# Modulation rows on the vector engine, and a written order in attention

## The chip, the cores and the metric

The kernel runs on one core of a Trainium2 chip. The core has five engines that work side by side, each on its own stream of instructions: TensorE (PE), which multiplies matrices and transposes, VectorE (DVE), ScalarE (ACT), GpSimd (POOL), and SyncE (SP), which issues the loads and stores. The metric is the device time of one execution in microseconds.

## The reference, cut to what matters

One layer over 1024 latent tokens of width 1024, with a context of 256 tokens. A conditioning vector gives six modulation rows; the layer is windowed attention beside a short convolution, an output projection with a gated residual, and a mixture of 16 experts in which each expert picks its 128 best tokens.

```python
mod = silu(c) @ w_ada + b_ada                     # six rows of 1024: sh1 sc1 gt1 sh2 sc2 gt2
h = rmsnorm(x, g_mix) * (1 + sc1) + sh1
q, k, v, bg, cg, hv = split(h @ w_in)
q, k = rope(q), rope(k)
att = softmax([sink, q @ k_ctx, q @ k_window] / 8) @ [v_ctx, v_window]
conv = bg * conv3(cg * hv)
x = x + gt1 * (concat(att, conv) @ w_out)
h2 = rmsnorm(x, g_ffn) * (1 + sc2) + sh2
x = x + gt2 * expert_choice_moe(h2)
out = rmsnorm(x, g_final)
```

## The kernel before, in words

**Stages.** First the rows sh1 and sc1 are computed for the latent and the context from 8 MB of `w_ada` (L230 on). Then the tokens are normalized and transposed and multiplied by the key/value weights, then by the query weights. Attention and the convolution run together; the output projection follows, tile by tile of 128 tokens, with the routing of the tile before beside it; then come the 16 experts, whose weights are 192 MB, and the last norm. Every fp32 operand of a large matrix product is split into a rounded high half and the rest as a low half, and three products of halves stand for one.

**Key/value and query projections.** `build_hT` (L281) transposes a strip of 128 columns of up to four token tiles on PE, applies the modulation and splits the result. For odd strips ACT applies the modulation and DVE makes both halves; for even ones DVE applies it, ACT makes the high half and POOL, or DVE for some, the low one (L289 to L297). `kv_stream` (L410) runs 24 builds, 8 for the context and 16 for the latent, and multiplies each strip three steps later (`proj_kv`, L311). `q_stream` (L524) then runs eight query tiles of 24 matmuls each (`q_proj`, L495); a tile's result is rotated (`rotary`, L320, lines 327 to 334, on DVE), its high half is made by ACT (L509) and its low half by DVE (L510). PE transposes a finished tile (`q_turn`, L513) behind the sixth step, that is the 18th matmul, of the next. The two streams of keys are transposed within the second tile (`turn_later`, L374).

**Later modulation rows.** Beside these projections `mod_stream` (L466) computes the other four rows, r = 0 to 3 for gt1, sh2, sc2 and gt2. For each row and each of 8 strips of the input it loads 512 KB of `w_ada`, ACT multiplies by the strip's silu values (L461) and POOL adds into a sum (L463). The sums over partitions are PE products with selecting columns (L473), and the four rows go to memory (L490).

**Attention.** A unit is one block of 128 queries and two heads, 32 units in all. `scores` (L551) multiplies, adds the mask while taking the maximum (L575), scales the maximum by -1/8 (L577), takes the exponential on ACT with its sum (L578), and treats the sink apart with small operations (L585 to L588) before it scales by the reciprocal (L592, L594). `values` (L599) transposes the probabilities of the unit before, splits them (L625, L626), multiplies them with the values and joins two halves of the result (ACT at L639, DVE at L643). `conv` (L714) runs 12 weight blocks of 16 steps; a block's weights are loaded one block ahead and split by ACT and POOL (L710, L711), and the three taps are computed on POOL and ACT (L755 to L760). `prepare` (L798) loads, gates and splits the first output weights.

**What sets the order.** `weave` (L69) takes the next piece of the stream that is furthest behind its share of a total, each yield being a piece's weight; that is the order in which instructions are written. PE executes as written everywhere. DVE, ACT, POOL and SP are ordered by a planner with its own simulated clock, except in stretches that are marked as written by hand, the end of the output projection for one. Every engine takes its instructions one after another: one that waits holds those behind it.

**Memory.** A pool of 21 large slots is handed out by `slots.get` and `slots.put`; a load waits for the last reader of its slot. Tiles named `wm` have three buffers in turn.

## Time and profile before

| | |
|---|---|
| median of 3 runs | 1163.87 us (1163.16 to 1164.9) |
| profiled execution | 1163.48 us, span 1161.7 us |
| PE, DVE, ACT, POOL busy | 91%, 83%, 66%, 30% of the span |
| granted clock, mean | 0.965 |
| DMA | 292.89 MB, mean 252 GB/s |

The span runs from the first to the last instruction; 1.78 us lie around it. Busy shares are means over stages. The granted clock is a share of TensorE's full speed of 2.4 GHz; its other level, 0.50, is 1.2 GHz. The page shows it by slices of 29 us:

```profile
PE   6786889999899998999399999999999999999981
DVE  7888455887878785389899999999999999999975
POOL 0457681221303031222212433322333322330022
PEclk9897999999999999999599999999999999999996
GB/s 376 232 164 144 164 146 19 24 33 1 55 1 37 19 278 339 181 127 270 273 322 356 399 403 390 391 388 389 395 404 392 389 389 389 394 404 390 203 195 221
```

Each digit is a busy share in tenths. The first slices are the modulation and the projections, the seventh to the fourteenth attention, the fifteenth to the nineteenth the output projection, the rest the experts and the end.

### The profile page before, as it was taken

How to read it: one execution, taken by the hardware profiler on the slowest of the kernel's cores; microseconds unless marked ns; L12 is line 12 of the kernel's file. 1: busy time of each engine (PE TensorE's matmuls, PEld its weight loads, DVE VectorE, ACT ScalarE, POOL GpSimd, SP SyncE). 2: the span in 40 equal slices, each digit the busy share in tenths (PEclk: the TensorE clock that was granted, in tenths of full speed). 3: DMA queues.
4: the chain of work that ended last, by engine and by line, in shares of the span. 5: the costliest groups of instructions: out<-in, count | busy, mean ns of one | idle time of the engine just before them, and what ended most of it. 6: DMA issues, size and time to landing. Idle time of an engine off the chain costs nothing.

```text
span 1161.7 us, 15615 instructions
## 1 busy us (share of the span) xinstructions
PE 1058.4 (91%) x5486; PEld 873.5 (75%) x5486; DVE 967.2 (83%) x1661; ACT 766.1 (66%) x1058; POOL 351.0 (30%) x292
## 2 busy tenths in 40 slices
PE   6786889999899998999399999999999999999981
PEld 2675667888788877888288888888888888888861
DVE  7888455887878785389899999999999999999975
ACT  7565655767666643232288878878878877888853
POOL 0457681221303031222212433322333322330022
PEclk9897999999999999999599999999999999999996
DMA  9644440010101079648789999999999999999555
GB/s 376 232 164 144 164 146 19 24 33 1 55 1 37 19 278 339 181 127 270 273 322 356 399 403 390 391 388 389 395 404 392 389 389 389 394 404 390 203 195 221
DMA packets 90790, 292.89 MB, mean 252 GB/s; under 512 B 7044, under 2 KB 20816, under 8 KB 89688
## 3 DMA queue, kind: packets, MB, share of 16 engines
q1 hardware_dynamic: 84808, 270.40, 61.0%
q0 software_dynamic: 5904, 21.50, 7.7%
q8 instruction: 43, 0.70, 0.2%
q14 instruction: 35, 0.29, 0.1%
HBM read 266.69 MB, written 25.18 MB: 251 GB/s over the span
## 4 chain that ended last, share of the span: by engine, by line
PE 72%; DVE 13%; issue 5%; ACT 4%; DMA 4%; POOL 1%; POOLq 0%; ACTq 0%; DVEq 0%; SPq 0%
PE pg L1313 14%; PE pu L1313 14%; PE py L1313 13%; PE po L879 7%; PE ps_cv L731 3%; PE ps_cv L730 3%; PE ps_cv L732 3%; PE pt L622 2%; PE po_att L613 2%; DVE whl L1150 2%; PE ps_s L565 2%; PE xTp L1299 1%; PE ps_s L563 1%; PE pl L954 1%; PE hTtp L1299 1%
## 5 line engine op out<-in xcount | busy, mean ns | idle before, releaser
L1150 DVE TENSOR_TENSOR whl<-raw,whl 128x1024 fp32r<-128x1024 f32 x384 | 455.2, 1224 | 29.9 <-ACT whl L1147 18.9
L1147 ACT CAST whl<-raw 128x1024 fp32r<-128x1024 f32 x384 | 400.2, 1054 | 100.2 <-PE pu L1313 35.6
L1313 PE MATMUL pg<-whl,xT 128*128 128x512 f32 x768 | 186.2, 395 | 2.1 <-DVE whl L1150 2.1
L1313 PE MATMUL pu<-whl,xT 128*128 128x512 f32 x768 | 180.9, 392 | 0.0
L1313 PEld LDWEIGHTS pg<-whl,xT 128*128 128x128 f32 x768 | 142.3, 189 | 31.6 <-DVE whl L1150 2.9
L1313 PE MATMUL py<-whl,hTt 128*128 128x512 f32 x720 | 165.9, 389 | 0.0
L1313 PEld LDWEIGHTS pu<-whl,xT 128*128 128x128 f32 x768 | 143.0, 188 | 29.4
L1313 PEld LDWEIGHTS py<-whl,hTt 128*128 128x128 f32 x720 | 135.1, 188 | 28.4 <-DVE whl L1150 0.3
L1278 POOL TENSOR_SCALAR oh<-iota,pos 128x128 bf16<-128x128 f32 x104 | 100.5, 981 | 0.5
L1371 POOL DMA_INDIRECT acc_d<-yt,idx x15 | 38.5, 2565 | 196.0 <-DVE yt L1359 196.0
L1323 POOL DMA_INDIRECT xr<-h_d,idx x16 | 22.3, 1395 | 199.2 <-DVE gate_w L1289 199.2
L730 PE MATMUL ps_cv<-hTh,wcs 128*128 128x512 f32 x192 | 81.5, 424 | 0.0
L463 POOL TENSOR_TENSOR acc<-acc,wmod 128x1024 f32<-128x1024 f32 x28 | 70.0, 2518 | 27.8 <-ACT wmod L461 26.7
L625 ACT CAST pth<-pt 128x512 fp32r<-128x512 f32 (+1 forms) x88 | 46.1, 524 | 46.2 <-PE pt L622 46.1
L731 PE MATMUL ps_cv<-hTl,wcs 128*128 128x512 f32 x192 | 76.1, 397 | 0.0
L732 PE MATMUL ps_cv<-hTh,wcs 128*128 128x512 f32 x192 | 76.0, 396 | 0.0
L879 PE MATMUL po<-woh,ah 128*128 128x512 f32 x240 | 70.8, 404 | 0.6 <-ACT woh L223 0.6
L626 DVE TENSOR_TENSOR pth<-pt,pth 128x512 fp32r<-128x512 f32 (+1 forms) x88 | 53.9, 613 | 20.1 <-ACT pth L625 19.2
L711 POOL TENSOR_TENSOR wcs<-wcr,wcs 128x1024 fp32r<-128x1024 f32 x12 | 28.6, 2389 | 110.2 <-ACT wcs L710 87.5
L578 ACT ACTIVATE sm<-sm,negm 128x640 f32<-128x640 f32 (+1 forms) x64 | 51.6, 807 | 4.0 <-DVE negm L577 3.9
L575 DVE CUSTOM_DVE_ANT_0 sm<-ps_s,maskt,sink 128x640 f32<-128x640 f32 (+1 forms) x56 | 48.3, 863 | 6.9 <-PE ps_s L565 6.3
L879 PEld LDWEIGHTS po<-woh,ah 128*128 128x128 f32 x240 | 44.1, 191 | 9.4 <-ACT woh L223 1.0
(297 smaller groups left out, 1828.4 us busy)
## 6 DMA issues: line engine op xcount, KB each, us to landing
raw<-in_w_gate_dram SPq DMA_DIRECT2D x64, 1024.0 KB, 9.6
raw<-in_w_up_dram SPq DMA_DIRECT2D x64, 1024.0 KB, 7.8
raw<-in_w_down_dram SPq DMA_DIRECT2D x64, 1024.0 KB, 9.6
wmod<-in_w_ada_dram SPq DMA_DIRECT2D x32, 512.0 KB, 3.7
wa<-in_w_ada_dram SPq DMA_DIRECT2D x8, 1024.0 KB, 5.3
wcr<-in_w_in_dram SPq DMA_DIRECT2D x12, 512.0 KB, 3.8
xt<-in_x_dram SPq DMA_DIRECT2D x4, 1024.0 KB, 20.6
wor<-in_w_out_dram SPq DMA_DIRECT2D x4, 1024.0 KB
```

Source lines behind the costliest of these rows:

```text
L463: nc.gpsimd.tensor_tensor(acc, acc, wt, op=OP.add)
L575: nc.vector.tensor_tensor_reduce(dst, src, mk, op0=OP.add, op1=OP.max, scale=1.0, scalar=sink8[:, h:h + 1], accum_out=mx[:, b, h:h + 1])
L578: nc.scalar.activation(sm, sm, AF.Exp, bias=negm[:, b, h:h + 1], scale=0.125, accum_out=esum[:, b, h:h + 1])
L626: nc.vector.tensor_tensor(pth[:, 1, :n], pt[:, :n], pth[:, 0, :n].bitcast(F32), op=OP.subtract)
L730: mm(ps, wsp[:, 0, k], hi, start=k == 0, stop=False)
L731: mm(ps, wsp[:, 0, k], lo, start=False, stop=False)
L732: mm(ps, wsp[:, 1, k], hi, start=False, stop=k == KC - 1)
L879: mm(po[n], a, wo[k // 4, n][j][:, k % 4], start=first, stop=last)
L1147: nc.scalar.copy(w[:, 0], t[:, k % 2])
L1150: low = nc.vector.tensor_tensor(w[:, 1], t[:, k % 2], w[:, 0].bitcast(F32), op=OP.subtract)
L1278: nc.gpsimd.tensor_scalar(oh[:, t], iota1, pos[:, t, 0, e:e + 1], None, op0=OP.is_equal)
L1313: mm(ps[n], a_hl[:, a, k], w[:, j, n * 512:(n + 1) * 512], start=first, stop=last)
```

## The change: what it does

The four later rows are computed with one DVE instruction per piece, which multiplies by the strip's silu value and adds to the sum (`mod_add`); POOL and ACT no longer take part. The four are taken apart: sh2 and sc2 stay beside the projections (`mod_stream`), each of their 16 loads with a dependence on the low half of the last finished query tile; gt1 is computed within attention in 24 pieces of 384 or 256 columns, summing in PSUM (`mod_attention`); gt2 is computed in the output projection of tiles 1 to 4, in 16 pieces of 512 columns (`last_row`). The sums over partitions are products with a column of ones, and the bias is added to a column form (`mod_sums`, `mod_row`); sc2's row already holds (1 + sc2) g_ffn.

In the projections, ACT now does both the modulation and the high half of every build, and DVE the low half; the low halves of the key/value weights move from POOL to DVE. The queries are scaled by -1/8 in the instructions of their split, so that attention takes a minimum and no scaled copy. In attention the sink is a further column of the scores, so its operations apart fall away; the join of a unit is written behind the first scores of the unit after the next; DVE and ACT now run as written, as PE does. The convolution's weights are split in halves between the steps of the block before, by ACT and DVE, and the taps are one ACT and two DVE instructions; POOL has no part in either. The first output weights are loaded apart from their gating.

```diff
@@ -265,7 +266,7 @@
     for i in range(2):
         ks = slice(4 * i, 4 * i + 4)
         nc.scalar.copy(wkv_h[:, ks], wkv_r[:, ks])
-        nc.gpsimd.tensor_tensor(wkv_l[:, ks], wkv_r[:, ks], wkv_h[:, ks].bitcast(F32), op=OP.subtract)
+        nc.vector.tensor_tensor(wkv_l[:, ks], wkv_r[:, ks], wkv_h[:, ks].bitcast(F32), op=OP.subtract)
@@ -286,15 +287,9 @@
...
+        nc.scalar.activation(hf, ps[:, :n], AF.Identity, scale=mscale[:, k, j:j + 1], bias=mshift[:, k, j:j + 1])
+        nc.scalar.copy(hi, hf)
+        nc.vector.tensor_tensor(lo, hf, hi.bitcast(F32), op=OP.subtract)
@@ -451,43 +446,94 @@
...
+    def mod_add(src, k, acc, out=None):
+        if k == 0:
+            nc.vector.tensor_scalar(acc, src, silu_c[:, 0:1], None, op0=OP.mult)
+        else:
+            nc.vector.scalar_tensor_tensor(acc if out is None else out, src, silu_c[:, k:k + 1], acc, op0=OP.mult,
+                                           op1=OP.add)
...
+    def mod_sums(pr, acc, r, k0=0):
+        n = acc.shape[1] // 128
+        for q in range(n):
+            mm(pr[:, q:q + 1], acc[:, q * 128:(q + 1) * 128], ones_f, start=True, stop=True)
+        c = 8 * r + k0
+        v = modv[:, c:c + n]
+        nc.vector.tensor_tensor(v, pr[:, 0:n], badaT[:, c:c + n], op=OP.add)
+        if r == 2:
+            nc.vector.scalar_tensor_tensor(v, v, 1.0, gffnT[:, k0:k0 + n], op0=OP.add, op1=OP.mult)
...
+    def mod_row(pr, r):
+        nc.tensor.transpose(pr[:8, :128], modv[:, 8 * r:8 * r + 8], ident)
+        row = w4("prow", (128,))
+        nc.scalar.copy(row[:8], pr[:8, :128])
+        nc.sync.dma_start(rows_d[r].rearrange("(k p) -> k p", p=128), row[:8])
...
+    def mod_stream():
...
+        yield 22
+        acc, s_acc = slots.get((2, D), F32, "acc")
...
+        for i in range(len(items) + 2):
+            if i < len(items):
+                k, r = items[i]
+                st_[i] = wm("wmod")
+                ld = mod_load(st_[i], r, k, slice(0, D))
+                if q_split:
+                    tc.add_manual_dep(ld.ins, q_split[-1].ins.name,
+                                      mybir.DependencyInfo(mybir.DependencyClass.Sync, mybir.DependencyReason.DATA),
+                                      reason="order")
+            if i > 1:
+                k, r = items[i - 2]
+                mod_add(st_.pop(i - 2), k, acc[:, r - 1])
             yield 1
...
+        yield 1
+        pr = p2(0, "prow")
+        for r in (1, 2):
+            mod_sums(pr[:, r - 1], acc[:, r - 1], r)
+        slots.put(s_acc)
+        for r in (1, 2):
+            mod_row(pr[:, r - 1], r)
...
+    def mod_attention(accp):
...
+        stage = work.tile([128, 2, 384], F32, tag="early", name="stage")
+        cols = (slice(0, 384), slice(384, 768), slice(768, 1024))
+        items = [(n, k) for n in range(3) for k in range(KC)]
...
+        yield 4
+        for i, (n, k) in enumerate(items):
+            w = cols[n].stop - cols[n].start
+            src = stage[:, i % 2, :w]
+            last = k == KC - 1
+            mod_add(src, k, accp[:, :w], src if last else None)
+            if last:
+                yield 1
+                mod_sums(accp, src, 0, cols[n].start // 128)
+            load(i + 2)
+            yield 1
+        mod_row(p1(3, "prow"), 0)
@@ -506,9 +552,12 @@
...
+        nc.scalar.activation(qs[:, :, 0, :], tv, AF.Copy, scale=-0.125)
+        low = nc.vector.scalar_tensor_tensor(qs[:, :, 1, :], tv, -0.125, qs[:, :, 0, :].bitcast(F32), op0=OP.mult,
+                                       op1=OP.subtract)
         qs_of[t] = qs
+        q_split.append(low)
...
-    weave([(urgent(steps(kv_stream(), q_stream())), 95.0), (mod_stream(), 56.0)])
+    weave([(urgent(steps(kv_stream(), q_stream())), 95.0), (mod_stream(), 42.0)])
@@ -554,7 +602,15 @@
...
+        def exp(i):
+            h = 2 * hp + i
+            sx = sm2[:, i, :W + 1]
+            nc.scalar.activation(sx, sx, AF.Exp, bias=mx[:, b, h:h + 1], scale=-1.0,
+                                 accum_out=esum[:, b, h:h + 1])
@@ -572,20 +628,17 @@
...
-            nc.vector.tensor_tensor_reduce(dst, src, mk, op0=OP.add, op1=OP.max, scale=1.0,
+            if i == 0:
+                nc.vector.tensor_copy(sm2[:, :, W], sink8[:, hs])
+            nc.vector.tensor_tensor_reduce(dst, src, mk, op0=OP.add, op1=OP.min, scale=1.0,
                                            scalar=sink8[:, h:h + 1], accum_out=mx[:, b, h:h + 1])
-            nc.vector.tensor_scalar(negm[:, b, h:h + 1], mx[:, b, h:h + 1], -0.125, None, op0=OP.mult)
-            nc.scalar.activation(sm, sm, AF.Exp, bias=negm[:, b, h:h + 1], scale=0.125,
-                                 accum_out=esum[:, b, h:h + 1])
             if i == 0:
-                yield
...
-        r = rec[:, b, hs]
-        nc.vector.tensor_tensor(r, sinkb[:, hs], negm[:, b, hs], op=OP.add)
-        nc.scalar.activation(r, r, AF.Exp)
-        nc.vector.tensor_tensor(r, r, esum[:, b, hs], op=OP.add)
-        nc.vector.reciprocal(r, r)
+                exp(0)
+            yield
+        exp(1)
+        yield
+        nc.vector.reciprocal(rec[:, b, hs], esum[:, b, hs])
@@ -633,16 +688,20 @@
...
+        def join():
...
+            up = work.tile([64, 2, 128], F32, tag="up", name="up")
+            nc.scalar.copy(up.rearrange("p b c -> p (b c)"), po[64:128])
+            pov = po.rearrange("p (b c) -> p b c", b=2)
+            for par in range(2):
+                dst = attT[b // 4][0][64 * par:64 * par + 64, hp, (b % 4) * 128:(b % 4 + 1) * 128]
+                nc.vector.tensor_tensor(dst, pov[:64, par], up[:, par], op=OP.add)
...
+        joined.append(join)
@@ -687,12 +736,24 @@
...
+            next(sc, None)
+            while joined:
+                joined.pop()()
+            yield 1
+            next(va, None)
+            yield 1
+            next(sc, None)
+            yield 1
+            next(va, None)
+            next(sc, None)
+            yield 1
+            if u == 0:
+                yield 1
+            next(va, None)
+            next(sc, None)
+            yield 1
+            next(va, None)
+        joined.pop()()
@@ -700,24 +761,33 @@
...
+        if i < 12:
...
+            raw = wm("wcr", (8, 128))
+            c0 = conv_col[part] + f * 128
+            nc.sync.dma_start(raw, win_v[:, :, c0:c0 + 128])
+            conv_w_of[i] = [raw, *slots.get((2, 8, 128), F32R, "wcs")]
+    def conv_split(i, low, n):
+        if i < 12:
+            raw, wsp, _ = conv_w_of[i]
+            ks = slice(4 * n, 4 * n + 4)
+            if low:
+                nc.vector.tensor_tensor(wsp[:, 1, ks], raw[:, ks], wsp[:, 0, ks].bitcast(F32), op=OP.subtract)
+            else:
+                nc.scalar.copy(wsp[:, 0, ks], raw[:, ks])
@@ -730,7 +800,16 @@
...
+                    at = 8 * half + k
+                    if at in (7, 8, 9, 10):
+                        conv_split(i + 1, *divmod(at - 7, 2))
+                    if part == 2 and at in (1, 4):
+                        j = 1 if at == 1 else 2
+                        nc.vector.scalar_tensor_tensor(st["y"], st["u"][:, j:j + S], convT_w[:, 4 * j + f:4 * j + f + 1],
+                                                       st["y"], op0=OP.mult, op1=OP.add)
+                    if k < KC - 1:
+                        yield 1
@@ -751,13 +831,7 @@
...
-                nc.gpsimd.tensor_scalar(y, u[:, 0:S], convT_w[:, f:f + 1], None, op0=OP.mult)
-                tap = wm("tap", (S,))
-                for j in (1, 2):
-                    w = convT_w[:, 4 * j + f:4 * j + f + 1]
-                    nc.scalar.activation(tap, u[:, j:j + S], AF.Copy, scale=w)
-                    nc.gpsimd.tensor_tensor(y, y, tap, op=OP.add)
+                nc.scalar.activation(y, st["u"][:, 0:S], AF.Copy, scale=convT_w[:, f:f + 1])
@@ -800,19 +881,25 @@
...
+        wo_issue(0)
+        yield 5
+        wo_issue(1)
+        wo_gate(0)
+        attended(0, ((0, 4),))
         yield 4
         wo_split(0)
...
+        yield 5
+        wo_issue(2)
+        wo_gate(1)
+        attended(0, ((4, 2),))
+        yield 4
         wo_split(1)
...
-        wo_load(2)
...
+    pb = p2(1, "po_att")
+    with tc.manual_schedule(engines={ET.PE, ET.DVE, ET.Activation}):
+        weave([(steps(attention(), prepare()), 160.0), (conv(), 161.0), (mod_attention(pb[:, 1]), 45.0)])
@@ -829,9 +916,6 @@
...
-    gf = wm("gf")
-    bcast_row(gf, g_ffn[0])
-    nc.vector.scalar_tensor_tensor(S2, S2, 1.0, gf, op0=OP.add, op1=OP.mult)
@@ -1183,6 +1267,33 @@
...
+    def last_row():
+        mem, s_ = slots.get((4, 512), F32, "gt2")
+        items = [(n, k) for n in range(2) for k in range(KC)]
...
+        for i in range(3):
+            load(i)
+        yield 6
+        for i, (n, k) in enumerate(items):
+            mod_add(mem[:, 1 + i % 3], k, mem[:, 0])
+            load(i + 3)
+            if k == KC - 1:
+                yield 1
+                mod_sums(p1(1, "prow"), mem[:, 0], 3, 4 * n)
+            yield 1.8
+        mod_row(p1(1, "prow"), 3)
+        slots.put(s_)
@@ -1190,13 +1301,22 @@
...
+    def last_row_part():
+        c = 0.0
+        while c < 10:
+            w = next(lrow)
+            c += w
+            yield w
...
-        beside(t, [[0.0, before(t)]])
+        lr = [[0.0, last_row_part()]] if 1 <= t < 5 else []
+        beside(t, [[0.0, before(t)]] + lr)
```

## Rows read from the trace of the kernel before

**Rows 1.** Windows view: stretch, us, busy PE, PEld, DVE, ACT, POOL, PEclk, DMA share, GB/s.

```profile
44.50:91.40 46.90, 39.64 (x287) 36.57 (x286) 38.76 (x49) 29.47 (x45) 23.50 (x14) 0.93 0.45 146
91.40:172.80 81.40, 63.96 (x288) 49.38 (x287) 50.19 (x71) 45.71 (x63) 59.06 (x25) 0.92 0.50 162
178.50:420.00 241.50, 234.21 (x1405) 201.94 (x1406) 184.65 (x503) 160.80 (x342) 48.20 (x20) 0.99 0.12 38
420.00:455.00 35.00, 31.52 (x135) 25.40 (x134) 30.91 (x26) 14.20 (x19) 9.33 (x5) 0.95 0.92 350
455.00:540.00 85.00, 85.00 (x455) 72.20 (x453) 54.67 (x258) 23.04 (x54) 22.91 (x46) 1.00 0.62 173
```

**Rows 2.** The waits view, 91.4 to 172.8 us: total, times, longest, in us.

```profile
PE pq L520 <- DVE qs L510: 13.1, 5, 4.6
```

**Rows 3.** The timeline of DVE, query stage: start, us, line, operation.

```profile
128.91 2.60 DVE L334 TENSOR_TENSOR t<-t 128x256 f32<-128x256 f32 x1
132.19 2.07 DVE L510 TENSOR_TENSOR qs<-t,qs 128x512 fp32r<-128x512 f32 x1 [0.68 <-ACT qs L509]
150.39 0.41 DVE L334 TENSOR_TENSOR t<-t 128x256 f32<-128x256 f32 x1
162.07 0.69 DVE L510 TENSOR_TENSOR qs<-t,qs 128x512 fp32r<-128x512 f32 x1 [0.74 <-ACT qs L509]
```

**Rows 4.** The timeline of POOL over the first two of those instructions.

```profile
126.29 7.42 POOL L463 TENSOR_TENSOR acc<-acc,wmod 128x1024 f32<-128x1024 f32 x3 [5.72 <-ACT wmod L461]
```

**Rows 5.** The lines view by form, 55 to 195 us: busy, mean ns, idle before.

```profile
L463 POOL TENSOR_TENSOR acc<-acc,wmod 128x1024 f32<-128x1024 f32 x28 | 70.0, 2518 | 27.8 <-ACT wmod L461 26.7 <-PE ps_q L503 0.5 <-ACT vx L343 0.5
```

**Rows 6.** The same view, 44.5 to 91.4 us, steps of the transposed build.

```profile
L290 ACT ACTIVATE hfs<-ps_xt,mshift,mscale 128x512 f32<-128x512 f32 x4 | 3.1, 776 | 0.0
L296 ACT CAST hTh<-hfs 128x512 fp32r<-128x512 f32 x4 | 2.4, 610 | 5.7 <-DVE hfs L294 5.7
L202 ACT ACTIVATE junk<-xt 128x1024 f32<-128x1024 f32 x3 | 3.2, 1056 | 0.3 <-POOL hcTl L297 0.3
L292 DVE TENSOR_TENSOR hTl<-hfs,hTh 128x512 fp32r<-128x512 f32 x4 | 5.1, 1285 | 0.1
```

**Rows 7.** The timeline of all engines, 30 to 37 us.

```profile
30.40 5.07 POOL L268 TENSOR_TENSOR wkvl<-wkvr,wkvh 128x1024 fp32r<-128x1024 f32 x2 [0.88 <-ACT wkvh L267]
31.14 2.08 DVE L254 TENSOR_TENSOR pmTv<-mparts 128x32 f32<-128x32 f32 x1
36.52 0.69 PE L286 MATMUL ps_xt<-ident,cxt 128*128 128x128 f32 x2 [4.71 <-DVE hf L294]
```

**Rows 8.** The timeline of PE, query stage.

```profile
162.81 1.09 PE L520 MATMUL pq<-ident,qs 128*128 128x128 f32 x8 [2.59 <-DVE qs L510]
163.66 0.48 PE L501 MATMUL ps_q<-wqh,hTh 128*128 128x512 f32 x1
164.21 0.39 PE L503 MATMUL ps_q<-wqh,hTl 128*128 128x512 f32 x1
164.44 0.40 PE L501 MATMUL ps_q<-wqh,hTh 128*128 128x512 f32 x1
```

**Rows 9.** The lines view by form, attention, 178 to 425 us.

```profile
L577 DVE TENSOR_SCALAR negm<-mx 128x1 f32<-128x1 f32 x64 | 9.8, 152 | 2.0
L585 DVE TENSOR_TENSOR rec<-sinkb,negm 128x2 f32<-128x2 f32 x32 | 9.0, 282 | 1.0
L587 DVE TENSOR_TENSOR rec<-rec,esum 128x2 f32<-128x2 f32 x32 | 12.0, 376 | 5.2 <-ACT rec L586 4.5
L626 DVE TENSOR_TENSOR pth<-pt,pth 128x512 fp32r<-128x512 f32 x64 | 44.1, 690 | 19.4 <-ACT pth L625 18.5
```

**Rows 10.** The waits of DVE, attention.

```profile
DVE attT L643 <- ACT up L639: 10.4, 15, 1.5
```

**Rows 11.** The page's costliest groups and its DMA issues.

```profile
L1150 DVE TENSOR_TENSOR whl<-raw,whl 128x1024 fp32r<-128x1024 f32 x384 | 455.2, 1224 | 29.9 <-ACT whl L1147 18.9
wmod<-in_w_ada_dram SPq DMA_DIRECT2D x32, 512.0 KB, 3.7
```

More of the change, by code (lines that the diff above doesn't have):

```diff
@@ L597, in tile_layer @@
     ptf = [0]
+    joined = []
     def values(u):
@@ L634, in values @@
             flush()
-        if b // 4 not in attT:
-            attT[b // 4] = slots.get((4, 512), F32, "attT")
-        up = work.tile([64, 2, 128], F32, tag="up", name="up")
-        nc.scalar.copy(up.rearrange("p b c -> p (b c)"), po[64:128])
-        pov = po.rearrange("p (b c) -> p b c", b=2)
-        for par in range(2):
-            dst = attT[b // 4][0][64 * par:64 * par + 64, hp, (b % 4) * 128:(b % 4 + 1) * 128]
-            nc.vector.tensor_tensor(dst, pov[:64, par], up[:, par], op=OP.add)
-        if b % 2 and hp == 3:
-            slots.put(qT[b // 2][1])
+        def join():
+            if b // 4 not in attT:
+                attT[b // 4] = slots.get((4, 512), F32, "attT")
+            up = work.tile([64, 2, 128], F32, tag="up", name="up")
[4 more added lines that the diff above has]
+                nc.vector.tensor_tensor(dst, pov[:64, par], up[:, par], op=OP.add)
+            if b % 2 and hp == 3:
+                slots.put(qT[b // 2][1])
+        joined.append(join)
     rt = {}
@@ L1184, in order_now, with load @@
         yield
+    def last_row():
+        mem, s_ = slots.get((4, 512), F32, "gt2")
+        items = [(n, k) for n in range(2) for k in range(KC)]
+        def load(i):
+            if i < len(items):
+                n, k = items[i]
+                mod_load(mem[:, 1 + i % 3], 3, k, slice(n * 512, n * 512 + 512))
+        for i in range(3):
[5 more added lines that the diff above has]
+            if k == KC - 1:
+                yield 1
+                mod_sums(p1(1, "prow"), mem[:, 0], 3, 4 * n)
+            yield 1.8
+        mod_row(p1(1, "prow"), 3)
+        slots.put(s_)
+        while True:
+            yield 99
+    lrow = last_row()
     def before(t):
```

154 lines of the change are left out of this document (49 added, 105 removed).

## The prediction

> **What bounds the kernel now.** I read the windows by stage first, then PE's waits, then the timelines of DVE and POOL where PE waits. The reader is to see three kinds of stretch. Beside the key/value and query projections PE is busy for 39.64 of 46.9 and 63.96 of 81.4 us, at a granted clock of 0.93 and 0.92; it falls to 1.2 GHz after the idle stretches [rows 1]. In attention it is busy for 234.21 of 241.5 us, in the output projection for 85.00 of 85.0. So only the projections have much to give, some 25 us of idle PE and the slow clock besides; attention has 7.3 us, the transition behind it 3.5.
>
> The waits say what holds the queries: PE's transposes of a finished query stand for its low half on DVE, 13.1 us in 5 waits [rows 2]. The timelines say why that half is late. The same additions and subtractions take 0.41 and 0.69 us in one query, 2.60 and 2.07 in another [rows 3], and over the long ones POOL runs three additions of the modulation rows [rows 4], 28 of them at 2518 ns [rows 5]. The same shows ahead of the stage: a DVE addition of 32 columns takes 2.08 us while POOL subtracts for 5.07, and PE then stands 4.71 us [rows 7].
>
> **The change part by part.** Terms are for the profiled execution, 1163.48 us (span 1161.7 and 1.78 around it), 0.39 under the median of 1163.87.
>
> *Start.* The key/value weights' low halves move from POOL to DVE. Their two subtractions of 1024 columns cost DVE 2 x 1.22 us [rows 11], behind the modulation's small operations, so those get their short durations back: about 4 us of the 4.71 [rows 7]. That does not pass through, because ACT now does both steps of every transposed build. With 0.78 and 0.61 us for 512 columns [rows 6], I estimate two thirds of 1.39, 0.9 us, for the context's 256. Eight of them and eight squares of 1.06 [rows 6] are 15.7 us from about 31.9 (4 us ahead of the build that feeds PE at 36.52), so the latent builds reach ACT at 47.6, and PE's transposes lead that by 1.6: 46, which is 1.5 later than the 44.5 of now.
>
> *Key/value projection, 44.5 to 91.4.* DVE keeps one subtraction per build (now 1285 ns where POOL is beside it [rows 6], else 0.69 [rows 3]); POOL has none and the modulation adds start later. ACT's builds come to 16 x 1.39 = 22.2 us, under PE's work. PE at 2.4 GHz: a transpose takes (163.66 - 162.81)/8 = 0.106 us, a 512-column matmul 0.23 from start to start [rows 8], a 256-column one half of it, 0.115. Sixteen builds of 4 transposes and 12 matmuls are 28.9 us, the last three context steps 2.1, eight key transposes 0.85: 31.9. Of today's 7.3 us of idle PE I leave 4, for ACT's chain. End: 46 + 31.9 + 4 = 82, against 91.4.
>
> *Query projection.* PE has 192 matmuls (43.9), seven turns of 8 transposes (6.0) and 32 key transposes (3.4), 53.3 us. The next query's 18 matmuls before a turn cover 4.1 us. Without POOL the chain of a query is two products from PSUM at 0.69 (the PSUM form of [rows 9]), two additions at 0.41 [rows 3], 0.61 on ACT [rows 6] and 0.69: 3.5 us and some handing over, so it just fits. New on DVE are 16 multiply-adds of 1024 columns; the trace has none, the nearest row of the same size is 1.22 us [rows 11], and I bound one between 0.7 (a 512-column form [rows 9]) and 2.5 (POOL's). Replaying the two streams by their yields puts load 0 in query 1, load 15 in query 6 and the last add in query 7, two or three per query. A rotary or a subtraction that finds one ahead of it is late by up to 1.2, so I take 0.9 per turn, 6 us in seven; and 5 for the key transposes, asked for 8 us after the last projection while DVE works through four key blocks. If all is hidden this is 0, if every turn meets two adds it is 17. Stage: 82 + 53.3 + 11 = 146.3.
>
> The tail to the first score takes 5.7 us now, from the end of the query window at 172.8 to 178.5. Then it is 16 one-column matmuls, two small additions, two transposes and two copies in a row, each waiting on the one before; I keep 5 (bounds 2 and 9). Attention starts at 151.3: **-27.2**. On SP each load stands behind a query's split and holds what is queued behind it, the next load and lastly the first convolution weights; these are wanted only behind the first score.
>
> One rule speaks against this part. The Trainium skill (Perfetto Trace Analysis, Optimizing Scalar/DVE Operations) says that work of a saturated DVE can go to ScalarE or even GpSimd, and warns that the port these two share may spoil it. Taken by its first half, bringing 16 adds of 1.22 us back would lift DVE's 50.19 us in the query stage [rows 1] to 69.7, about 5 us over the stage forecast, and the sum would be 1143. The trace sides with the warning: most of a long subtraction was time spent beside POOL [rows 3, 4].
>
> *Attention, 178.5 to 420.* DVE loses 64 scalings of the maximum (9.8 us) and two small operations per unit (9.0 and 12.0): 30.8 [rows 9]. It gains 24 weight subtractions of 512 columns at 0.69 (16.6), 8 convolution taps at 1.22 (9.8), 32 sink columns at 0.15 (4.8) and 24 adds of row 0, which I take at 0.5 between a small form's 0.15 and 0.69 (12): 43.2. Net +12 on 184.65 of 241.5 us [rows 1], so DVE has room; ACT's count hardly moves. PE's gain is at most its 7.3 us idle. Against that DVE and ACT now run as written: the joining additions stand for ACT's copy, and that copy behind an exponential (today 10.4 us in 15 waits, longest 1.5 [rows 10]). Bounds -6 and +40; I take **+2**, nearest to today's waits. Loads of row 0 have 10 us each to land in 3.7 [rows 11].
>
> *Transition, 420 to 455.* Output weights are loaded a step ahead of their gating and splitting; PE idles 3.5 us here [rows 1]. Bounds -3.5 and +3: **-2**.
>
> *Output projection, 455 to 540.* PE has no idle here, so each of its waits counts. It gains 8 one-column matmuls and a transpose; DVE gains 16 adds of 512 columns, 16 x 0.69 = 11 on 54.67 of 85 us. Their loads, 256 KB each, go through SP among the expert weights, at a DMA share of 0.62, three ahead. Hidden under PE's matmuls; if a load is late, PE stands at one of two sums and DVE at its add, with the residual queued behind. Bounds 0 and +15: **+1**. The expert stage's own code is not touched; it only moves.
>
> *At nothing.* Some 40 more lines of 512 B among the first small loads are 0.1 us at the 376 GB/s of the first slice. The query's factor and sign ride in instructions that are there anyway. One row less is loaded and multiplied behind attention (1.2 us of DVE, beside PE's first projection).
>
> Sum: 1163.48 - 27.2 + 2 - 2 + 1 = 1137.3, some 1138 on the scale of the median.
>
> **The rivals.**
> *Full cover.* PE never waits beside the projections: 46 + 31.9 + 53.3 + 5 = 136.2, which is -42.3; with -3.6 in attention and -3.5 behind it, 1114. For it: 3.5 of chain under 4.1 of cover, and no POOL. Against: 16 adds in the same DVE stream.
>
> *Late loads hold DVE.* An add whose load is released only by the query's split waits for landing, 3.7 us [rows 11], and the rotary stands behind it: 3.7 in place of 0.9 in seven turns is 19.6 more, 1157. For it: DVE takes its instructions one after another. Against: each add is written two loads behind its own load.
>
> *Attention becomes DVE's (slower).* Per unit of 33, DVE has 196.9/33 = 5.97 us of work. If it also stands 1.5 for the copy behind the exponential [rows 10], 0.6 for the transposed probabilities (today 18.5 us over 33 [rows 9]) and 0.5 for the second exponential before its reciprocal, a unit takes 8.57 against PE's 7.32: +41 us, 1176. It loses to today from 8.2 us a unit. For it: the written order. Against: PE runs ahead only as far as two buffers, and now waits little.
>
> *The moved rows collide.* Row 3's loads land late between 1 MB weight loads, and PE pays the +15 above: 1151.
>
> **How the numbers follow.** Forecast 0.64, full cover 0.13, late loads 0.12, slower attention 0.06, collision 0.05. 1118 to 1158 leaves out the slower case and about half of the full cover. A measurement of this kernel can tell about 0.2%, 2.3 us. All cases but the slower attention lie below that bound; for thin margins of late loads I put 0.03 on no change: faster 0.91, same 0.03, slower 0.06.
>
> **What would show it.** The first score near 151 us with POOL nearly idle before it, the subtraction of the queries at 0.69 in all eight, a granted clock near 1.00 between 82 and 146, and attention still 240 to 246 us long confirm the steps. A wait of DVE's multiply-add for its load in most queries shows the late loads; PE idle of more than 15 us in attention, released by DVE, shows the slower case. The forecast is wrong if attention starts later than 160 or takes over 255.

## The result, and the profile after

The changed kernel takes 1208.78 us (median of 4 runs, 1205.17 to 1211.85) against 1163.8 for the kernel before on the same chip: ratio 1.0384, interval 1.0354 to 1.0414. It is slower, and the forecast of 1138 was wrong in sign.

I cut both profiled executions (1205.17 us with a span of 1203.4, which is 3.6 us under its median; 1163.48 with 1161.7) at the same events. Times in us:

| stretch | before | after | difference |
|---|---|---|---|
| to the last key/value product | 90.8 | 86.3 | -4.5 |
| to the last query product | 81.6 | 73.8 | -7.8 |
| to the first score | 6.1 | 6.7 | +0.6 |
| attention, to the first output product | 255.2 | 299.3 | +44.1 |
| output projection | 116.6 | 126.9 | +10.3 |
| routing, experts, last norm | 611.4 | 610.4 | -1.0 |

The windows of the changed kernel follow, from its first transpose of a latent tile; columns as in [rows 1]. The last line is attention in the kernel before, cut at the same events.

```profile
46.30:86.30 40.00, 35.98 (x284) 34.68 (x284) 22.23 (x36) 30.53 (x52) 1.20 (x2) 0.96 0.14 51
86.30:160.10 73.80, 59.36 (x282) 48.39 (x282) 45.33 (x86) 20.02 (x39) 0.00 (x0) 0.93 0.38 128
166.80:466.10 299.30, 265.18 (x1481) 222.87 (x1482) 194.27 (x465) 161.91 (x321) 2.24 (x13) 0.96 0.17 55
178.50:433.70 255.20, 247.91 (x1466) 213.26 (x1467) 197.96 (x509) 164.93 (x345) 56.76 (x23) 0.99 0.15 50
```

POOL is empty beside the query projections, as meant, and yet PE idles there for 14.4 us at a clock of 0.93. In attention PE, DVE and ACT all idle, PE for 34 us: none of them is full, so they stand for each other. Of the 44.1 us that attention lost, 26.8 are idle PE and 17.3 a PE that is busy for longer, at a granted clock of 0.96 where it had 0.99. The waits of attention (166.8 to 466 us) say where:

```profile
ACT sm L611 <- DVE mx L634: 75.6, 51, 3.9
DVE attT L700 <- ACT up L696: 42.1, 32, 1.4
...
ACT pth L680 <- PE pt L677: 24.3, 26, 3.5
```

Before, ACT stood mostly for PE's transposes, and the copy for the joining additions cost DVE 10.4 us [rows 10]. ACT's wait before, 178.5 to 433.7 us:

```profile
ACT pth L625 <- PE pt L622: 46.1, 50, 2.5
```

Now ACT stands at its exponentials for DVE's maximum. A unit has two of them, one per head: 51.8 of the 75.6 us stand at the first and 23.8 at the second. The timeline of ACT, and then that of DVE, show a first exponential at 217.45, a second at 223.71 and the first of the next unit at 229.97:

```profile
217.45 0.83 ACT L611 ACTIVATE sm<-sm,mx 128x641 f32<-128x641 f32 x1 [1.36 <-DVE mx L634]
...
218.40 0.37 ACT L696 COPY up<-po_att 64x256 f32<-64x256 f32 x1
...
219.85 1.08 ACT L680 CAST pth<-pt 128x512 fp32r<-128x512 f32 x2
223.71 0.83 ACT L611 ACTIVATE sm<-sm,mx 128x641 f32<-128x641 f32 x1 [2.79 <-DVE mx L634]
...
224.54 0.35 ACT L680 CAST pth<-pt 128x256 fp32r<-128x256 f32 x1
...
229.97 0.83 ACT L611 ACTIVATE sm<-sm,mx 128x641 f32<-128x641 f32 x1 [3.63 <-DVE mx L634]
```

```profile
218.80 0.58 DVE L700 TENSOR_TENSOR attT<-po_att,up 64x128 f32<-64x128 f32 x2 [1.39 <-ACT up L696]
...
221.07 0.61 DVE L457 SCALAR_TENSOR_TENSOR po_att<-stage,silu_c,po_att 128x384 f32<-128x384 f32 x1
221.60 1.28 DVE L809 SCALAR_TENSOR_TENSOR cg<-u,smallT,cg 128x1024 f32<-128x1024 f32 x1
222.79 0.88 DVE L634 CUSTOM_DVE_ANT_0 sm<-ps_s,maskt,sink 128x640 f32<-128x640 f32 x1
...
224.93 0.42 DVE L681 TENSOR_TENSOR pth<-pt,pth 128x256 fp32r<-128x256 f32 x1 [0.64 <-ACT pth L680]
...
225.93 0.62 DVE L457 SCALAR_TENSOR_TENSOR po_att<-stage,silu_c,po_att 128x384 f32<-128x384 f32 x1
...
229.04 0.88 DVE L634 CUSTOM_DVE_ANT_0 sm<-ps_s,maskt,sink 128x640 f32<-128x640 f32 x1 [1.24 <-PE ps_s L621]
```

For the second exponential the scores were ready, but DVE had an addition of row 0 and a convolution tap ahead of the maximum. So that exponential came at 223.71, and the 0.35 us copy of transposed probabilities behind it only at 224.54, though PE had made the transposes (0.44 us from 221.21) nearly three microseconds earlier. DVE's subtraction, an addition of row 0 and then PE's value products followed in a chain. PE's timeline has the end of it:

```profile
221.21 0.44 PE L677 MATMUL pt<-ident,sm 128*128 128x128 f32 x2 [0.47 <-DVE pth L681]
...
226.69 1.25 PE L668 MATMUL po_att<-pth,vx 128*128 128x256 f32 x6 [3.45 <-DVE po_att L457]
```

PE multiplies the next scores only behind these products, so the next maximum came at 229.04 and the first exponential that stands for it at 229.97. Behind a first exponential, as at 217.45, wait the joining copy (218.40), at which DVE then stands with all its later work (218.80), and the first copies of transposed probabilities (219.85).

Beside the query projections the rows read otherwise. DVE waits for the loads of its additions, and PE for the low halves of the queries (waits, 86.3 to 160.1 us):

```profile
DVE acc L457 <- DMA wmod<-in_w_ada_dram: 10.3, 5, 3.9
...
PE pq L569 <- DVE qs L557: 14.4, 7, 3.9
```

One turn in DVE's timeline, and the transposes of PE that it releases:

```profile
107.38 0.69 DVE L557 SCALAR_TENSOR_TENSOR qs<-t,qs 128x512 fp32r<-128x512 f32 x1
112.01 1.29 DVE L457 SCALAR_TENSOR_TENSOR acc<-wmod,silu_c,acc 128x1024 f32<-128x1024 f32 x1 [3.94 <-DMA wmod<-in_w_ada_dram]
113.21 0.68 DVE L322 TENSOR_TENSOR t<-ps_q,ropet 128x512 f32<-128x512 f32 x1
...
114.41 1.28 DVE L457 SCALAR_TENSOR_TENSOR acc<-wmod,silu_c,acc 128x1024 f32<-128x1024 f32 x1
115.60 0.42 DVE L328 TENSOR_TENSOR t<-t 128x256 f32<-128x256 f32 x1
...
116.27 1.28 DVE L457 SCALAR_TENSOR_TENSOR acc<-wmod,silu_c,acc 128x1024 f32<-128x1024 f32 x1
117.47 0.68 DVE L557 SCALAR_TENSOR_TENSOR qs<-t,qs 128x512 fp32r<-128x512 f32 x1
```

```profile
118.30 1.94 PE L569 MATMUL pq<-ident,qs 128*128 128x128 f32 x8 [3.55 <-DVE qs L557]
```

Two or three loads are released by one split and land together; DVE stands for the first with the rotary behind it, and the other two additions sit inside the rotary. The window from 110 us is the landing, at a DMA share of 0.94. PE's idle then costs clock (windows of 4 us): 0.59 is a mixture of the levels 1.2 and 2.4 GHz, and the eight transposes above take 1.94 us where a turn at full clock takes 1.06.

```profile
110.00:114.00 4.00, 4.00 (x19) 3.29 (x19) 1.99 (x3) 0.00 (x0) 0.00 (x0) 1.00 0.94 357
114.00:118.00 4.00, 0.75 (x4) 0.29 (x2) 4.00 (x6) 0.63 (x1) 0.00 (x0) 0.99 0.01 2
118.00:122.00 4.00, 3.70 (x14) 3.33 (x15) 0.15 (x1) 1.17 (x2) 0.00 (x0) 0.59 0.66 228
```

### The profile page after: what moved, and what is told of

The parts are those of the page before. It is cut to its first block, busy times and chain, and to the rows that moved or that the text cites. A ratio compares the mean times of both kernels' runs of the same rounds, so it can differ in the third digit from the quotient of the medians.

```text
span 1203.4 us, 15590 instructions
## 1 busy us (share of the span) xinstructions
PE 1074.5 (89%) x5537; PEld 887.1 (74%) x5537; DVE 952.6 (79%) x1640; ACT 744.0 (62%) x1030; POOL 204.6 (17%) x228
## 4 chain that ended last, share of the span: by engine, by line
PE 65%; DVE 16%; ACT 7%; issue 6%; DMA 5%; POOL 1%; POOLq 0%; SPq 0%; DVEq 0%; ACTq 0%
PE pg L1433 15%; PE pu L1433 14%; PE py L1433 13%; PE po L963 5%; PE po_att L668 2%; DVE sm L634 2%; ACT sm L611 2%; DMA wmod<-in_w_ada_dram 2%; PE ps_cv L800 2%; PE ps_cv L801 2%; PE ps_cv L802 2%; DMA gt<-in_w_ada_dram 2%; DVE pth L681 1%; PE ps_s L621 1%; DVE acc L457 1%
## 5 line engine op out<-in xcount | busy, mean ns | idle before, releaser
L611 ACT ACTIVATE sm<-sm,mx 128x641 f32<-128x641 f32 (+1 forms) x64 | 51.6, 807 | 77.1 <-DVE mx L634 75.6
L800 PE MATMUL ps_cv<-hTh,wcs 128*128 128x512 f32 x192 | 83.1, 433 | 0.0
L802 PE MATMUL ps_cv<-hTh,wcs 128*128 128x512 f32 x192 | 77.5, 403 | 0.0
L681 DVE TENSOR_TENSOR pth<-pt,pth 128x512 fp32r<-128x512 f32 (+1 forms) x88 | 54.0, 616 | 18.5 <-ACT pth L680 17.4
L677 PEld LDWEIGHTS pt<-ident,sm 128*128 128x128 f32 x304 | 39.0, 144 | 18.0 <-DVE pth L681 5.8
L700 DVE TENSOR_TENSOR attT<-po_att,up 64x128 f32<-64x128 f32 x64 | 18.1, 283 | 42.5 <-ACT up L696 42.1
```

The costliest lines, as they stand in the source:

```text
L611: nc.scalar.activation(sx, sx, AF.Exp, bias=mx[:, b, h:h + 1], scale=-1.0, accum_out=esum[:, b, h:h + 1])
L681: nc.vector.tensor_tensor(pth[:, 1, :n], pt[:, :n], pth[:, 0, :n].bitcast(F32), op=OP.subtract)
L800: mm(ps, wsp[:, 0, k], hi, start=k == 0, stop=False)
L802: mm(ps, wsp[:, 1, k], hi, start=False, stop=k == KC - 1)
```

## The experiments

Ratios are to the kernel before, with 95% intervals. "Stage" is the query stage up to the last query product, "attention" and "output" as in the table. Attention was not edited in e5, e6 and e7, and their profiles show 302.2, 299.3 and 304.6 us for it beside the 299.3 of the changed kernel; so a difference of 5 us in it, from one profile each, is not clear of noise.

**Attention ordered by the planner** (e1_planner), only PE as written.

```diff
-    with tc.manual_schedule(engines={ET.PE, ET.DVE, ET.Activation}):
+    if True:
```

> The changed kernel with one edit: in attention DVE and ACT are ordered by the planner again, PE as written. Measured so far, from the first score to the first output product: 255.2 us before, 299.3 in the changed kernel. Theory W (the written order makes DVE and ACT stand for each other; 38 us of DVE waits for the joining copy): the stage falls to about 250 to 260, the whole to about 1165. Theory L (what was added to DVE there, or the sums of row 0 in PE's memory, is the cost): the stage stays at 290 or more, the whole at 1200 or more.

1169.24 us, 1.0044 (1.0023 to 1.0066). Attention 266.0, output 123.6. The written order costs 33.3 of attention's 44.1 us, nearest to Theory W, and 3.3 of the output's 10.3.

**The join ahead of the scores** (e2_join_first), all as written.

```diff
-            next(sc, None)
             while joined:
                 joined.pop()()
+            next(sc, None)
```

> The changed kernel with one edit: the join of a unit is written ahead of the first scores of the unit after the next instead of behind them, so ACT's joining copy no longer stands behind an exponential; order still as written. Theory W in its narrow form (that one place is the cost): DVE's waits for the copy fall from 38 to under 15 us and the stage by 20 to 35, to 265 to 280. Theory W in its wide form (the whole order): the stage falls by under 10. Theory L: no change beyond 5 us.

1209.3, 1.038 (1.0315 to 1.0445); attention 301.4. No gain. But the wait that was to go did not: from 166.7 to 468 us DVE still stands 34.1 us in 30 waits for the joining copy, where it stood 42.1 in 32, and its wait for the probabilities' copy grew from 17.4 to 56.1. So this run does not say what the joining copy costs, only that this place for it is no better.

**Row 0 left out** (e3_row0_out: its loads, additions and sums, so its values are the bias alone), and **row 0 summed in SBUF** (e4_row0_own_sums) in 32 pieces of 256 columns, not in the PSUM tile of the value products.

```diff
-            mod_add(src, k, accp[:, :w], src if last else None)
+            mod_add(src, k, stage[:, 2], src if last else None)
```

> The changed kernel without the loads and multiply-adds of row 0 in attention (the row is the bias alone). Takes away 24 DVE instructions of 0.5 to 0.6 us, 14 us of 300. Theory L: PE's waits for row 0's adds go and the stage falls by 20 us or more, to 280 or less. Theory W: it falls by the DVE time at most, 5 to 14 us, to 285 to 295.

> The changed kernel with row 0 summed in the main memory, beside its two load buffers, instead of in the matrix engine's memory beside the attention result; pieces of 256 columns, 32 instead of 24. If it is the place of the sums that makes PE's products wait for row 0's adds (3.5 us in one unit), these waits go and the stage falls by 8 to 15 us, to 284 to 291. If it is DVE's order alone, it stays within 5 us of 299, since DVE has the same work in the same places.

e3: 1177.95, 1.0111 (1.0081 to 1.014), attention 269.5. e4: 1190.67, 1.022 (1.019 to 1.025), attention 283.8. In the written order row 0's 13.7 us of DVE cost 29.8 of attention; by its numbers e3 is the case of Theory L, while e1 comes nearest to Theory W. Half of the 29.8 (15.5) goes when the sums leave the shared tile: PE's value products no longer wait for them. DVE's wait for ACT's copy stays at 42.1 us in both, so that wait, the largest of DVE's, is not by itself the loss.

**Without the hold on the loads** (e5_no_gate), and **rows 1 and 2 left out** (e6_rows12_out; their values are the bias alone).

```diff
-                if q_split:
-                    tc.add_manual_dep(ld.ins, q_split[-1].ins.name, ...)
```

> The changed kernel without the dependence of each load of rows 1 and 2 on a query's split; three buffers alone hold the loads back. The query projection took 81.6 us before and 73.8 in the changed kernel, where PE's own work is about 53. Theory G (loads let go only by the split land too late, and DVE stands at a multiply-add with the rotary behind it): the query stage falls to 58 to 66, the whole to about 1195. Theory D (DVE's 16 more multiply-adds are the cost, loaded or not): it stays within 4 us of 74.

> The changed kernel without the loads and multiply-adds of rows 1 and 2 beside the query projections (these rows are the bias alone). It bounds what these 16 pieces cost in all: by both theories the query stage falls to 54 to 60 us, and it shows what the stage costs with no modulation row on any engine. If it stays above 66, neither the loads nor the adds are the cost, and the chain of a query itself is.

e5: 1203.96, 1.0322 (1.0286 to 1.0358); stage 70.7. The additions crowd into 86 to 112 us, DVE busy for 24.30 of 25.7 there; behind them PE is busy for 44.56 of 45. DVE hardly stands for the loads any more (1.3 us in the stage), and yet the stage is only 3.1 us shorter: by its numbers this is Theory D, the additions themselves. e6: 1182.38, 1.0137 (1.0108 to 1.0167); stage 55.6, first score at 142.9. Its window of that stage:

```profile
86.50:142.70 56.20, 54.64 (x289) 45.71 (x288) 29.18 (x72) 21.46 (x44) 0.00 (x0) 1.00 0.00 1
```

Without the rows PE hardly idles and the clock stays at 1.00. The two rows cost 80.5 - 55.8 = 24.7 us of stage and tail, for 19.4 us of additions (14 at 1.28 and 2 at 0.75).

**Row 3 left out** (e7_row3_out; bias alone).

> The changed kernel without the loads and multiply-adds of row 3 in the output projection (the row is the bias alone). From the first to the last output product: 116.6 us before, 126.9 in the changed kernel. If row 3's adds, with the residual behind them, are the cost, this falls by 4 to 10 us. If it is the start of the stage, where PE stands 12 us for the first split weights, it falls by under 2.

1204.23, 1.0324 (1.0271 to 1.0378); output 121.7. Row 3 costs 5.2 of its 10.3 us. With the 3.3 of the written order, 1.8 are left, if the two add up.

**Planner and own sums** (e10_planner_own_sums).

> The changed kernel with the planner's order in attention (266.0 us there instead of 299.3) and row 0 summed in main memory (283.8 with the written order). If the two costs are of one kind, PE's products held by row 0's adds, the second edit adds little: 262 to 266. If they are separate, attention falls to about 250 to 256, the stage's length before, and the whole to 1153 to 1158, below the kernel before.

1170.22, 1.0045 (1.0031 to 1.0059); attention 268.2. Under the planner own sums gain nothing: in e1 no wait of PE for row 0's additions is left to remove, and in e10 DVE stands 7.9 us for the loads of the smaller pieces.

**Planner, row 0 left out** (e12_planner_row0_out), **planner, earlier loads** (e13_planner_earlier_loads), **rows 1, 2 and 0 in attention** (e14_rows_in_attention), **the builds alone in the kernel before** (e15_builds_alone).

```diff
-                if q_split:
-                    tc.add_manual_dep(ld.ins, q_split[-1].ins.name, ...)
+                if len(q_split) > 1:
+                    tc.add_manual_dep(ld.ins, q_split[-2].ins.name, ...)
```

> The changed kernel with attention ordered by the planner and row 0's loads, additions and sums left out (its values are the bias alone). With the planner and row 0 attention took 266.0 us, before the change 255.2. If row 0 is what is left of the loss, attention comes to 254 to 258 us and the ratio to about 0.995 (8 to 12 us under the planner's 1.0044). If the loss is the other work given to DVE there (24 weight subtractions, 8 taps, 32 sink columns), attention stays at 262 to 266 us and the ratio at 1.00 or above.

> The changed kernel with attention ordered by the planner, and each load of rows 1 and 2 held by the split of the query before the last, not of the last. With the planner alone the query stage took 72.4 us, without the two rows 55.6. If what the rows cost is the wait of their additions for loads that land late (10.3 us of DVE), that wait goes to under 3 us, the stage comes to 62 to 66 us and the ratio to 0.995 to 0.999. If it is the additions' own 20 us on DVE ahead of the rotaries, the stage stays at 69 to 73 and the ratio at 1.002 to 1.006.

> The changed kernel with attention ordered by the planner and rows 1 and 2 computed in attention too, ahead of row 0, in the same pieces of 384 and 256 columns (72 additions in place of 24, about 27 us more of DVE, which is busy for 196 of 264 us there); the router's constants move from units 20 to 23 to units 27 to 30. The query stage should come to 55 to 57 us and the first score to 143 to 145. If DVE has room under PE in attention, that grows from 266 by 5 to 12 us and the ratio is 0.985 to 0.993, faster than both kernels. If attention is DVE's by then, it grows by 27 us or more, and the ratio is 1.005 or above.

> The kernel before with one part of the change alone: the low halves of the key/value weights on DVE, and every transposed build with both its steps on ACT and its subtraction on DVE. If that part is worth what the changed kernel shows up to the end of the key/value projection, this comes 3 to 6 us earlier (before 90.8, after 86.3), and the ratio is 0.995 to 0.998. If ACT, which here also scales the modulation rows, is late with the builds, nothing is gained up to there and the ratio is 1.000 or above.

e12: 1163.95, 0.9985 (0.9972 to 0.9997); attention 258.5, nearly the first case: row 0 costs 7.5 us under the planner, all else 3.3. e13: 1161.65, 0.9973 (0.9959 to 0.9988); stage 67.7, tail 6.8. It is some 3 us faster than the kernel before, and 47 than the changed one. It stands between the two cases: the waits for loads halved and did not vanish (waits of that stage):

```profile
DVE acc L457 <- DMA wmod<-in_w_ada_dram: 5.4, 3, 5.1
```

e14: 1163.82, 0.9989 (0.9979 to 0.9999); first score at 141.4, attention 287.6. The rows save 19.5 us ahead of attention against e13 and cost 21.9 in it, between the two cases. e15: 1164.53, 0.9999 (0.9987 to 1.0011); key/value products end at 92.5, not earlier. Alone the new builds gain nothing. The changed kernel is 4.5 us earlier there, and the rows say why. In e15 PE stands for the builds' low halves on DVE (30 to 94 us), 7.7 us where the changed kernel has 1.8, while its waits for the high halves on ACT are alike (1.5 and 1.3). And POOL still adds the modulation rows there: five of DVE's sixteen subtractions run beside it and take 2.46 to 2.87 us, the other eleven run beside nothing of POOL's and take 0.68 to 0.69. After that wait follow the lines by form, e15 from 40 to 92.5 us and the changed kernel from 40 to 86.3:

```profile
PE ps_kv L312 <- DVE hTl L291: 7.7, 6, 2.0
```

```profile
L291 DVE TENSOR_TENSOR hTl<-hfs,hTh 128x512 fp32r<-128x512 f32 x8 | 15.1, 1906 | 5.8 <-ACT hTh L290 5.8
```

```profile
L292 DVE TENSOR_TENSOR hTl<-hfs,hTh 128x512 fp32r<-128x512 f32 x8 | 5.4, 690 | 6.8 <-ACT hTh L291 6.8
```

So, by these rows, the builds pay only together with an idle POOL.

**One engine as written at a time** (e16_dve_as_written, e17_act_as_written).

```diff
-    with tc.manual_schedule(engines={ET.PE, ET.DVE, ET.Activation}):
+    with tc.manual_schedule(engines={ET.PE, ET.DVE}):              # e16
+    with tc.manual_schedule(engines={ET.PE, ET.Activation}):       # e17
```

> The changed kernel with DVE's order in attention as written and ACT's left to the planner. If it is DVE's written order that loses the time (joining additions and row 0's additions ahead of work that PE waits for), attention stays at 290 to 300 us and the ratio at 1.030 to 1.038. If it is ACT's, attention comes to 266 to 272 and the ratio to 1.005 to 1.010. If each costs a part of it, about 283.

> The changed kernel with ACT's order in attention as written and DVE's left to the planner. If DVE's written order is the cause, attention comes to 266 to 272 us and the ratio to 1.005 to 1.010. If ACT's is (the copy for the joining additions, or a second exponential, ahead of the probabilities' copy that PE waits for), attention stays at 290 to 300 and the ratio at 1.030 to 1.038.

e16: 1173.07, 1.0082 (1.0056 to 1.0108), attention 273.9. e17: 1194.59, 1.0249 (1.0218 to 1.028), attention 293.6. ACT's order alone costs 27.6 us over the planner's 266.0, DVE's alone 7.9: the attention of e17 lies in its second case, and e16 comes near its own. The waits of e16 and then of e17, 180 to 440 us:

```profile
ACT sm L611 <- DVE mx L634: 29.9, 29, 2.7
...
DVE attT L700 <- ACT up L696: 1.4, 3, 0.7
```

```profile
ACT sm L611 <- DVE mx L634: 66.4, 30, 5.3
...
DVE attT L700 <- ACT up L696: 30.2, 24, 1.4
```

**Rows of attention in own sums** (e18_rows_in_attention_own_sums) and **one row beside, two in attention** (e19_row1_beside), both by the planner.

> Rows 1, 2 and 0 in attention under the planner as in the run before, but in 96 pieces of 256 columns summed in SBUF and not in the other half of the value products' PSUM tile. There PE waited 11.3 us in 13 waits for those additions and attention took 287.6. If the shared tile is the cause, attention comes to 274 to 279 us and the ratio to 0.988 to 0.992. If DVE's time is (205 of 264 us busy), the 96 smaller additions, 46 us in place of 41, make it 290 to 295 and the ratio 1.002 or above.

> One row beside the query projections, its loads held by the split two queries back, and rows 2 and 0 in attention under the planner, 64 pieces of 256 columns summed in SBUF. If a row costs least where DVE has the most room left, eight additions beside the projections make that stage 58 to 61 us and attention is 272 to 277: ratio 0.986 to 0.992. If a row costs its 10 us of PE wherever it stands, the ratio is that of two rows beside the projections, 0.996 to 0.999.

e18: 1192.48, 1.0233 (1.0198 to 1.0268), attention 316.2. e19: 1172.79, 1.0074 (1.0047 to 1.01), stage 60.0, attention 286.3. Both worse than e14 and e13, and worse than either case of mine: with pieces of 256 columns and two loads ahead, the loads don't land in time. DVE stands 34.5 us for them in e18 and 20.0 in e19, where e14 has 6.1. So they don't settle what the shared tile costs with three rows.

**The convolution back on POOL** (e20_conv_on_pool, on e13), and **the exponential a step later** (e21_exp_later, the changed kernel, all as written).

```diff
+            yield
             if i == 0:
                 exp(0)
-            yield
         exp(1)
```

> The run with attention by the planner and the loads held by the split before the last (1161.65 us, ratio 0.9973, attention 265.7), with the convolution's weight subtractions and taps back on POOL and ACT as in the kernel before. If DVE's 24 subtractions and 8 taps are what is left of attention's loss beside row 0, attention comes to 257 to 261 us and the ratio to 0.989 to 0.993. If POOL beside DVE stretches row 0's additions and the subtractions that PE waits for, attention stays at 265 or grows, and the ratio is 0.997 or above.

> The changed kernel, all as written, but the first exponential of a unit is issued a step later, behind the copy for the joining additions and the first copy of the transposed probabilities. If attention is lost because that exponential stands on ACT for DVE's maximum (69 us of waits) with those copies behind it, DVE's wait for the copy falls from 39.6 us to under 15, attention from 299.3 to 270 to 280 and the ratio to 1.010 to 1.020. If it is DVE's work in written order (row 0 and the taps ahead of the maximum), ACT only stands elsewhere, attention stays at 293 to 303 and the ratio at 1.032 or above.

e20: 1165.25, 0.9992 (0.9977 to 1.0007), attention 264.1. DVE is busy for 186.89 us of it, in e13 for 196.83, and attention is only 1.7 us shorter: the convolution's work on DVE is not what costs. (POOL stretches a few of DVE's instructions there, one sink copy to 2.05 us, so a small gain could be hidden.) e21: 1174.92, 1.0084 (1.0069 to 1.0099), attention 271.4. Moving that one instruction, the first exponential of each unit, gives back 27.9 us. Its waits, 167 to 440 us, and its window of attention:

```profile
ACT pth L680 <- PE pt L677: 60.9, 57, 4.1
...
ACT sm L611 <- DVE mx L634: 5.4, 3, 3.9
...
DVE attT L700 <- ACT up L696: 1.6, 2, 1.3
```

```profile
166.30:437.70 271.40, 253.96 (x1481) 218.74 (x1482) 193.63 (x465) 157.86 (x321) 2.23 (x13) 0.98 0.19 61
```

ACT stands for PE again. Its waits for the maximum fall from 75.6 us to 5.4, and DVE's for the joining copy from 42.1 to 1.6. DVE's busy time is what it was (193.63 against 194.27): no work was saved, only standing.

## Why the prediction was wrong, point by point

*Attention, "+2", the step that failed.* Measured +44.1. It divides, run by run, into 27.9 for the place of the first exponential (299.3 to 271.4), 5.4 for the rest of the written order (to 266.0 in e1), 7.5 for row 0 (to 258.5 in e12) and 3.3 for all else (to 255.2). By the spread of 299.3 to 304.6 us between profiles, the 5.4 and the 3.3 are not clear of noise. The terms of DVE's work held: row 0's additions took 13.7 us where I had 12, and in this cut DVE is busy for 194.27 us, before for 197.96, as some of the output weights' work moved behind it (my 196.9 is for the shorter stretch to 420). What failed is the overlap: I took the value "nearest to today's waits" for it. The waits of [rows 10] were those of a planned order and could not bound a written one, in which ACT stood 75.6 us for DVE's maximum and DVE 42.1 for ACT's copy; the bound of +40 was the better end. The division depends on the order of the steps: with the exponential where it was, leaving out row 0 alone gives back as much (29.8 us, e3), since the additions ahead of the maximum and the copies behind the exponential are two ends of one chain.

*The rival "attention becomes DVE's".* I priced it at 8.57 us a unit and gave it 0.06; measured 299.3/33 = 9.07. Its 1.5 us for the copy behind the exponential appeared as 42.1 us in 32 waits, 1.3 each. But it was not DVE that became the bound: in e3 and e4 that wait stands unchanged while attention falls to 269.5 and 283.8. So that term alone is not the loss. Two copies stand behind the first exponential, the joining copy and the transposed probabilities that PE wants; e21 freed both at once, and e2 did not free the first, so which of them mattered more is not shown. I had argued that "PE runs ahead only as far as two buffers, and now waits little"; this says nothing of PE once ACT's order is fixed.

*First score, "-27.2".* Measured -11.7. The key/value end came at 86.3 where I had 82, the stage at 73.8 where I had 64.3, the tail at 6.7 where I had 5. In the key/value projection the start (46.3, forecast 46) and the idle PE (4.0 us, forecast 4) held; PE was busy for 36.0 us where I had 31.9, in part by a clock of 0.96. In the stage PE's work was right: e6, without the rows, shows 55.6 against my 53.3 without waits. That leaves 2.3 us where I had put 5 for the key transposes, and 18.2 for the rows where I had put 6. So "0.9 per turn" was the term that failed, and for two reasons. The smaller is the *late loads* rival: letting the loads go earlier gave back 4.7 us (e1 to e13) and not holding them 3.1 (e5). Most of the rest stays with the loads in time and goes with the additions, which stand on DVE ahead of the rotaries. The counter-argument to late loads, "each add is written two loads behind its own load", failed because one split releases two or three loads at once, so the add is behind loads of the same moment; a load took 6.6 us to landing (median of 16) in place of 3.7 [rows 11]. I left out too that PE's longer idle costs clock, 0.93 where I expected near 1.00. The part without POOL held: the stretched arithmetic of [rows 3, 4] is gone. The lines view of that stage, by form:

```profile
L457 DVE SCALAR_TENSOR_TENSOR acc<-wmod,silu_c,acc 128x1024 f32<-128x1024 f32 x14 | 17.8, 1280 | 10.3 <-DMA wmod<-in_w_ada_dram 10.3
...
L557 DVE SCALAR_TENSOR_TENSOR qs<-t,qs 128x512 fp32r<-128x512 f32 x7 | 4.8, 685 | 1.1 <-ACT qs L556 1.1
```

The price of a multiply-add, 1280 ns, was taken well (1.22).

*The rule of the Trainium skill (Perfetto Trace Analysis, Optimizing Scalar/DVE Operations)*, whose warning on the port shared by DVE and GpSimd I weighed there: these rows agree with the warning, with every subtraction of 512 columns near 0.69 us once POOL is idle. By its first half the 24.7 us that the two rows cost here could be had on another engine; no run put them on ScalarE with POOL idle, so that stays open.

*Transition and output projection, "-2" and "+1".* Measured +10.3 in this cut. Row 3 is 5.2 of it (e7), so the *collision* rival was right in kind and priced at three times its size. 3.3 go with the planner. The largest wait of PE there, at the start, is for the split of output weights, a wait that my -2 had taken to be gone. The waits of the stage, 466 to 593 us, PE and then DVE:

```profile
PE po L963 <- ACT woh L224: 6.0, 1, 6.0
...
DVE gt L457 <- DMA gt<-in_w_ada_dram: 8.7, 4, 3.9
```

*What nothing settles.* The 3.3 us of attention that stay without row 0 and under the planner, and the 1.8 of the output, were not taken apart, nor were the two copies behind the first exponential. That the exponential's move and the earlier loads add up was not run.

## What to carry to other kernels

When an engine's order changes from planned to written, its old waits are no estimate. Go through the written list and ask of each instruction that can stand (here an exponential that needs another engine's maximum) which ready, short instructions are queued behind it and who wants them: moving one such instruction was worth 27.9 us here, without an instruction saved. A load that is held by an event needs its landing time between that event and the first reader on an in-order engine, and loads released by one event land together.

## What the runs showed of the hardware that was not expected

Sixteen loads of 512 KB that were released in groups took 6.6 us to landing (median) where such loads spread out took 3.7 [rows 11]. The mean DMA share of that stage, 0.38, hides the crowding: in the 4 us in which one group landed it was 0.94, at 357 GB/s. Beside POOL's additions a subtraction of two operands in SBUF took 2.46 to 2.87 us where it takes 0.69 alone (e15), but 14 subtractions of attention in the kernel before, with one operand in PSUM, ran wholly beside POOL's work and took 0.69 us each. And the clock followed short idle: after a stretch with PE busy for 0.75 of 4 us the next 4 us were granted 0.59, though both neighbours were at 1.00 or near it.
